# A two-layer hybrid decoder trunk on one core: keys carried in DRAM, a fifth weight-pair tile, and a last output projection that goes block by block

## The chip, the cores and the metric

The kernel runs on one core of a Trainium2 chip. The metric is the device time of one execution in microseconds; the time before is the median of three runs. TensorE is called PE below, VectorE DVE, ScalarE ACT, GpSimd POOL, and SyncE SP. SP issues every DMA of this kernel, in one queue, in order.

## The reference, cut to what matters

Two layers run over 2048 positions of width 1024. In each layer the same input feeds sliding-window attention (16 query heads in 4 key/value groups, window 128) and a Mamba-2 chunked scan (16 heads in 2 groups, 128 states, chunks of 128 positions). Their outputs, each gated with SiLU, are concatenated and go through one output projection; the result is added to the scaled input and layer-normalised.

```python
def hybrid_layer(x, w_in, ..., w_out, ln_g, ln_b):
    proj = jnp.einsum("bld,de->ble", x, w_in)
    q, k, v, z_attn, z_ssm, xbc, dt_raw = jnp.split(proj, IN_SPLITS, axis=-1)
    attn = sliding_window_attention(q, k, v, sinks) * jax.nn.silu(z_attn)
    ...
    y = ssd_chunked(xs, dt, a, bm, cm)
    ...
    ssm = gated_rmsnorm(y, z_ssm, ssm_norm_w)
    out = jnp.einsum("ble,ed->bld", jnp.concatenate([attn, ssm], axis=-1), w_out)
    return layer_norm(DEEPNORM_ALPHA * x + out, ln_g, ln_b)
```

## The kernel before

**Chunks, halves, blocks.** A layer L goes through four chunks c of 512 positions. A chunk has two halves; each half does two of the four key/value groups and one of the two scan groups. Work on tokens goes in four blocks b of 128 positions.

**Parts and pairs.** Every float32 matmul operand is held as a high part and a low part in a 32-bit matmul format, and a product is three matmuls: high by high, high by low, low by high (lines 236 to 238, 244 to 246, 480 to 482). Both parts of a piece of a weight lie side by side in one tile, `wpair`, 4 KB for each partition; four of them rotate. A pair serves twelve matmuls of 512 columns. In layer 0 the parts are made on first use, or ahead of use by `w_ahead` for layer 1 (raw weights come into `wr`, the parts go out to DRAM); later uses load 512 KB of ready parts (`w_split`, line 126). The load can be issued only when the matmuls that read the tile's former content are done.

**Order of a half.** `stage_k` projects two groups of keys; `proj_a` projects queries and gates; the output projection of the half before that was put aside (`late`, `tail`) is flushed; `mix_a` does attention for one group, block by block, twice; `proj_s` projects the scan's inputs; `out_proj` projects the attention output (grp 0 or 1); `mix_s` runs the scan over the four blocks, one after the other because a state is carried; its output projection (grp 2 or 3) is `tail`. After the second half `norm_store` does the layer norm.

**The keys.** A `kt` tile holds the parts of one group's keys: 128 columns of the chunk before, then 512 of this one. There are two such tiles. The last 128 columns are copied by ACT into a tile that stays, `kcar` (line 327, the name `kc` in the trace), and copied back into the next chunk's tile by POOL (line 322).

**The mixer's tiles.** What `mix_a` and `mix_s` hand to the output projection are the parts in `mixt`, four tiles, one for each block. A `mix_s` block's tile is the one that the attention output of the same half had, so its content can be written (line 623) once both column halves dh of `out_proj` have read the block.

**The end.** For the last half of the last chunk of the last layer `tail` runs `out_proj` for the first 512 output columns of all four blocks (line 769, `dhs=1`), and then `last_out`: four pairs of the second column half are loaded, three of them into the query tiles `q`, which are free by then; for each block the twelve matmuls of the second half, the addition into `racc`, and the layer norm, whose statistics need both halves (lines 674 to 702). The factor `rstd` of the gated norm is made for all four blocks at once, after the last block of `mix_s` (lines 624 to 627).

**What sets the order.** The program is written in the order above, and a planner then orders each engine's instructions by a simulated timeline (line 44): of what is ready in its simulation, what stands earlier in the program goes first. On the chip each engine keeps that order, SP's queue of DMAs among them. So an instruction that is late on the chip holds up all that stands behind it on its engine, and a change of the number of tiles moves instructions everywhere.

**On-chip memory.** The four `kcar` tiles take 1 KB of a partition each, as much together as one `wpair` tile.

Of the kernel before, what the change touches and what calls it, by code (L numbers as in the profile page):

```python
# [31 lines left out]
P = 128  # L32
# [3 lines left out]
CH = 512  # L36
# [19 lines left out]
def trunk(ctx, tc, a):  # L56
# [16 lines left out]
    def bank(pool, name):  # L73
        if pool is ps_pj:
            return pool.tile([P, 512], F32, name=name, tag="bank")
        tag = TAG[name]
        return pool.tile([P, 512], F32, name=name, tag=tag, bufs=NS if tag == "s" else 1)
# [10 lines left out]
        nc.sync.dma_start(out=t if len(src.shape) == 2 else t.rearrange("p (k n) -> p k n", k=src.shape[1]), in_=src)  # L88
        return t

    kcar = [const.tile([P, 2, P], F32R, name=f"kc{i}") for i in range(4)]
    state = [const.tile([P, 512], F32, name=f"st{i}") for i in range(2)]
    halo = const.tile([P, 12, 3], F32, name="halo")

# [24 lines left out]
    def w_split(key, c, dsrc, n, scale=None, pool=False, dst=None):  # L119

        if dst is None:
            dst = wp.tile([P, 2, WP], F32R, name="wpair", bufs=4)
        d = dst[:, :, 0:n]
        hs, ls = d[:, 0], d[:, 1]
        if key in w_dram:
            nc.sync.dma_start(out=d.bitcast(F32), in_=w_dram[key])
            cnt["use"] += 1
            if cnt["use"] % 3 == 0 and ahead:
                w_ahead(*ahead.pop(0))
            return hs, ls  # L130
        src = w_load(dsrc, n)
        cnt["w"] += pool
        w_parts(hs, ls, src, scale, nc.gpsimd if pool and cnt["w"] % 2 == 0 else nc.vector)
        if key[1] > 0 or not on_use(key):
            nc.sync.dma_start(out=w_store(key, n), in_=d.bitcast(F32))
        return hs, ls
# [175 lines left out]
    def stage_k(L, c, pr, X):  # L312
        ps = bank(ps_cm, "ps_k")
        proj_cm(X, L, pr, ps, pool=False)
        kts = []
        for i in range(2):
            kv = 2 * pr + i
            kt = ap_.tile([P, 2, P + CH], F32R, name="kt", bufs=2)
            kf = kt.bitcast(F32)
            s, o = (slice(0, 64), slice(64, 128)) if i == 0 else (slice(64, 128), slice(0, 64))  # L320
            if c > 0:
                nc.gpsimd.tensor_copy(out=kt[:, :, 0:P], in_=kcar[kv].bitcast(F32))
            nc.scalar.copy(out=kt[s, 0, P:], in_=ps[s])
            nc.vector.tensor_tensor(out=kt[s, 1, P:], in0=ps[s], in1=kf[s, 0, P:], op=ALU.subtract)
            nc.scalar.copy(out=kt[o, 0, P:], in_=ps[s])
            nc.vector.tensor_copy(out=kt[o, 1, P:], in_=kf[s, 1, P:])
            nc.scalar.copy(out=kcar[kv], in_=kf[:, :, CH:CH + P])
            kts.append(kt)
        return kts

# [136 lines left out]
    def new_mixt():  # L467
        return [xp.tile([P, 2, 4, P], F32R, name="mixt", bufs=4) for _ in range(NB)]

    def out_proj(L, c, grp, mixt, racc, evac, nw=None, pre=None, dhs=2):  # L470
        for dh in range(dhs):
            if pre is not None:
                pre(dh)
            banks = [bank(ps_acc, "ps_out") for _ in range(NB)]
            for e in range(4):
                wh, wl = w_split(("o", L, grp, dh, e), c, a["wo"][L, grp, dh][:, e, :], 512,
                                 None if nw is None else nw[:, e:e + 1])
                for b in range(NB):
                    mh, ml = mixt[b][:, 0, e, :], mixt[b][:, 1, e, :]
                    nc.tensor.matmul(out=banks[b], lhsT=mh, rhs=wh, start=(e == 0), stop=False)  # L480
                    nc.tensor.matmul(out=banks[b], lhsT=mh, rhs=wl, start=False, stop=False)  # L481
                    nc.tensor.matmul(out=banks[b], lhsT=ml, rhs=wh, start=False, stop=(e == 3))  # L482
            for b in range(NB):
                evac(b, racc[b][:, dh * 512:(dh + 1) * 512], banks[b])
# [63 lines left out]
        o["zs"] = [silu2(banks[b], sp.tile([P, 512], F32, name="zss", bufs=4)) for b in range(NB)]  # L548
        return o

    def mix_s(L, lc, c, g, d, o, mixt):
        ssq = sm.tile([P, NB], F32, name="ssq")
        for b in range(NB):
            blk = slice(b * P, (b + 1) * P)
            hs = slice(b * 16 + g * 8, b * 16 + g * 8 + 8)
# [65 lines left out]
            for e in range(4):  # L621
                nc.tensor.transpose(out=pg[:, e * P:(e + 1) * P], in_=y[:, e * P:(e + 1) * P], identity=ident)
            split(mixt[b][:, 0], mixt[b][:, 1], pg.rearrange("p (e t) -> p e t", e=4), "act")
        rstd = sm.tile([P, NB], F32, name="rstd")
        nc.vector.tensor_scalar(out=rstd, in0=ssq, scalar1=1.0 / 2048, scalar2=EPS, op0=ALU.mult, op1=ALU.add)
        nc.gpsimd.tensor_tensor(out=rstd, in0=rstd, in1=mhalf, op=ALU.pow)
        nc.vector.tensor_scalar(out=rstd, in0=rstd, scalar1=0.5, scalar2=None, op0=ALU.mult)
        return rstd

    def norm_store(L, c, racc):  # L630
# [27 lines left out]
    def last_out(L, c, grp, mixt, racc, rstd, nw):  # L658

        gb = []  # L660
        for i in range(2):
            gb.append([])
            for n in ("lng", "lnb"):
                t = sp.tile([P, CH], F32, name="cacc", bufs=4) if i == 0 else wp.tile([P, 512], F32, name=n, tag="wr", bufs=4)
                nc.sync.dma_start(out=t, in_=a[n][L][:, i * 512:(i + 1) * 512])
                gb[i].append(t)
        w = []
        for e in range(4):
            w.append(w_split(("o", L, grp, 1, e), c, a["wo"][L, grp, 1][:, e, :], 512, nw[:, e:e + 1],
                             dst=ap_.tile([P, 2, CH], F32R, name="q", bufs=3) if e < 3 else None))  # L670
        for b in range(NB):
            r = racc[b]
            st = sm.tile([P, 2, 6], F32, name="bst")
            nc.vector.bn_stats(out=st[:, 0, :], in_=r[:, 0:512])
            ps = bank(ps_acc, "ps_out")
            for e, (wh, wl) in enumerate(w):
                mh, ml = mixt[b][:, 0, e, :], mixt[b][:, 1, e, :]
                nc.tensor.matmul(out=ps, lhsT=mh, rhs=wh, start=(e == 0), stop=False)
                nc.tensor.matmul(out=ps, lhsT=mh, rhs=wl, start=False, stop=False)
                nc.tensor.matmul(out=ps, lhsT=ml, rhs=wh, start=False, stop=(e == 3))  # L680
            ev_rstd(rstd)(b, r[:, 512:], ps)
            nc.vector.bn_stats(out=st[:, 1, :], in_=r[:, 512:])
            mv = sm.tile([P, 2], F32, name="bmv")
            nc.vector.bn_aggr(out=mv, in_=st)
            rs = sm.tile([P, 1], F32, name="brs")
            nc.vector.tensor_scalar(out=rs, in0=mv[:, 1:2], scalar1=EPS, scalar2=None, op0=ALU.add)
            nc.gpsimd.tensor_tensor(out=rs, in0=rs, in1=mhalf[:, 0:1], op=ALU.pow)
            nm = sm.tile([P, 1], F32, name="bnm")
            nc.vector.scalar_tensor_tensor(out=nm, in0=mv[:, 0:1], scalar=-1.0, in1=rs, op0=ALU.mult, op1=ALU.mult)
            for i in (1, 0):  # L690
                cs = slice(i * 512, (i + 1) * 512)
                h = r[:, cs]
                if i == 1:
                    nc.scalar.activation(out=h, in_=h, func=AF.Identity, scale=rs, bias=nm)
                    nc.gpsimd.tensor_tensor(out=h, in0=h, in1=gb[i][0], op=ALU.mult)
                    eng = nc.vector if b > 0 else nc.gpsimd
                    eng.tensor_tensor(out=h, in0=h, in1=gb[i][1], op=ALU.add)
                else:
                    nc.vector.scalar_tensor_tensor(out=h, in0=h, scalar=mv[:, 0:1], in1=gb[i][0], op0=ALU.subtract,
                                                   op1=ALU.mult)  # L700
                    nc.vector.scalar_tensor_tensor(out=h, in0=h, scalar=rs, in1=gb[i][1], op0=ALU.mult, op1=ALU.add)
                nc.sync.dma_start(out=a["out"][c * CH + b * P:c * CH + (b + 1) * P, cs], in_=h)
# [32 lines left out]
    for L in range(DEPTH):  # L735
# [3 lines left out]
        for c in range(NCH):  # L739
# [7 lines left out]
            for half in range(2):  # L747
# [12 lines left out]
                    Xn = XLoad(L + (c + 1) // NCH, (c + 1) % NCH)  # L760
                    pre = Xn.half
                out_proj(L, c, half, mixt, racc, ev_alpha if half == 0 else ev_add, pre=pre)
                mixt = new_mixt()
                rstd = mix_s(L, lc, c, half, d, o, mixt)

                def tail(L=L, c=c, half=half, mixt=mixt, racc=racc, rstd=rstd, lc=lc):
                    end = half == 1 and L == DEPTH - 1 and c == NCH - 1
                    nw = lc["nw"][:, half * 4:half * 4 + 4]
                    out_proj(L, c, 2 + half, mixt, racc, ev_rstd(rstd), nw, dhs=1 if end else 2)
                    if end:  # L770
                        last_out(L, c, 2 + half, mixt, racc, rstd, nw)
                    elif half == 1:
                        norm_store(L, c, racc)

                late.append(tail)
# [60 lines left out]
```

## Time and profile before

| what | us |
|---|---|
| median of 3 runs | 3191.21 |
| lowest and highest run | 3185.13, 3192.55 |
| the profiled execution, its own time | 3184.89 |
| its span, first to last instruction | 3182.9 |
| PE busy | 3079.0 (97%) |
| DVE, ACT, POOL busy | 2153.3, 1612.5, 1365.2 |
| granted TensorE clock, mean | 0.991 of full |

The profile is of one execution. Times in the trace count from its first instruction. PE's busy time is made of modelled ends, so that of matmuls that follow each other the steps from start to start count, and not the length of one. "Released by" stands for the instruction or DMA that ended a wait.

### The profile page before, as it was taken

What the parts mean: (1) busy time and instruction counts of PE and PEld (TensorE: products, weight loads), DVE (VectorE), ACT (ScalarE), POOL (GpSimd) and SP (SyncE); (2) the same over time, 40 slices, a digit from 0 to 9 for tenths busy, and PEclk for the clock granted to TensorE, in tenths of its full rate; (3) what the DMA queues carried; (4) which work ended last, traced back from release to release, by engine and by line L of the source; (5) the groups of instructions that cost most, each with busy time, mean ns of one, the idle gap of its engine ahead of it and who ended that gap; (6) DMA issues with size and microseconds to landing.
All of it is one profiled execution on the core that took longest, in us unless ns stands there. A gap on an engine that the chain in (4) does not pass through costs nothing.

```text
span 3182.9 us, 48382 instructions
## 1 busy us (share of the span) xinstructions
PE 3079.0 (97%) x15704; PEld 2577.9 (81%) x15704; DVE 2153.3 (68%) x4686; ACT 1612.5 (51%) x4599; POOL 1365.2 (43%) x1967
## 2 busy tenths in 40 slices
PE   8999999999998999999999999999999999999996
PEld 7878787878877788877888888888888888888885
DVE  5877768676686676866757676675766747666475
ACT  5746537455373553645536464372643636335362
POOL 2554534425354253542535434444344433455234
PEclk9999999999999999999999999999999999999998
DMA  8657759496594864957556556765556545575452
GB/s 312 233 189 247 248 172 318 150 316 211 170 322 145 289 228 155 326 188 268 189 159 226 176 193 190 229 201 166 180 173 235 183 159 185 168 229 181 152 196 79
DMA packets 254461, 663.58 MB, mean 208 GB/s; under 512 B 28288, under 2 KB 49408, under 8 KB 254208
## 3 DMA queue, kind: packets, MB, share of 16 engines
q1 hardware_dynamic: 254208, 660.49, 62.4%
q8 instruction: 124, 2.03, 0.3%
q14 instruction: 129, 1.06, 0.1%
HBM read 534.02 MB, written 126.35 MB: 207 GB/s over the span
## 4 chain that ended last, share of the span: by engine, by line
PE 71%; DMA 15%; DVE 5%; POOL 3%; ACT 3%; issue 2%; SPq 1%; DVEq 0%; ACTq 0%; POOLq 0%
PE ps_out L480 6%; PE ps_out L482 6%; PE ps_out L481 6%; PE ps_xbc L238 3%; PE ps_xbc L236 3%; PE ps_xbc L237 3%; PE ps_q L236 3%; PE ps_q L238 3%; PE ps_q L237 3%; PE ps_yd L581 3%; PE ps_z L238 3%; PE ps_z L236 3%; PE ps_z L237 3%; DMA wr<-wcm 3%; PE ps_zs L244 3%; PE ps_zs L245 2%
## 5 line engine op out<-in xcount | busy, mean ns | idle before, releaser
L480 PE MATMUL ps_out<-wpair,mixt 128*128 128x512 f32 x1008 | 395.4, 401 | 26.3 <-DMA wpair<-wd_o 13.3
L482 PE MATMUL ps_out<-wpair,mixt 128*128 128x512 f32 x1008 | 397.1, 396 | 7.2 <-DVE mixt L105 4.0
L481 PE MATMUL ps_out<-wpair,mixt 128*128 128x512 f32 x1008 | 396.8, 394 | 0.4 <-DVE wpair L105 0.4
L414 ACT ACTIVATE e<-e,nm 128x129 f32<-128x129 f32 x512 | 202.7, 397 | 219.5 <-DVE nm L410 218.9
L236 PE MATMUL ps_xbc<-xh,wpair 128*128 128x512 f32 x768 | 305.2, 397 | 0.6 <-DMA wpair<-wd_cm 0.5
L238 PE MATMUL ps_xbc<-xh,wpair 128*128 128x512 f32 x768 | 303.6, 395 | 0.0
L237 PE MATMUL ps_xbc<-xl,wpair 128*128 128x512 f32 x768 | 302.3, 394 | 0.0
L435 POOL TENSOR_SCALAR_AFFINE_SELECT gh<-fh 64x256 fp32r<-64x256 f32 x256 | 110.3, 431 | 333.4 <-ACT fh L100 325.0
L480 PEld LDWEIGHTS ps_out<-wpair,mixt 128*128 128x128 f32 x1008 | 191.0, 191 | 72.6 <-DMA wpair<-wd_o 17.2
L574 ACT ACTIVATE e<-e,nacs 128x128 f32<-128x128 f32 x512 | 163.7, 392 | 161.3 <-DVE e L572 155.0
L482 PEld LDWEIGHTS ps_out<-wpair,mixt 128*128 128x128 f32 x1008 | 191.3, 190 | 50.7 <-DVE mixt L105 6.3
L526 DVE SCALAR_TENSOR_TENSOR cacc<-ps_xbc,conv,cacc 128x511 f32<-128x511 f32 (+2 forms) x288 | 213.1, 740 | 23.5 <-ACT cacc L523 22.0
L481 PEld LDWEIGHTS ps_out<-wpair,mixt 128*128 128x128 f32 x1008 | 191.8, 190 | 38.7 <-DVE wpair L105 0.8
L244 PE MATMUL ps_zs<-wpair,xh 128*128 128x512 f32 x512 | 205.0, 403 | 8.5 <-DMA wpair<-wd_z 7.9
L236 PE MATMUL ps_q<-xh,wpair 128*128 128x512 f32 x512 | 201.4, 393 | 2.8 <-DMA wpair<-wd_cm 1.5
L246 PE MATMUL ps_zs<-wpair,xl 128*128 128x512 f32 x512 | 202.7, 397 | 0.0
L245 PE MATMUL ps_zs<-wpair,xh 128*128 128x512 f32 x512 | 202.6, 396 | 0.0
L236 PE MATMUL ps_z<-xh,wpair 128*128 128x512 f32 x512 | 201.8, 394 | 0.0
L238 PE MATMUL ps_z<-xh,wpair 128*128 128x512 f32 x512 | 201.7, 394 | 0.0
L238 PE MATMUL ps_q<-xh,wpair 128*128 128x512 f32 x512 | 200.5, 392 | 0.8 <-DVE wpair L105 0.8
L237 PE MATMUL ps_z<-xl,wpair 128*128 128x512 f32 x512 | 200.8, 392 | 0.0
L237 PE MATMUL ps_q<-xl,wpair 128*128 128x512 f32 x512 | 200.8, 392 | 0.0
(219 smaller groups left out, 8287.6 us busy)
## 6 DMA issues: line engine op xcount, KB each, us to landing
wpair<-wd_cm SPq DMA_DIRECT2D x420, 512.0 KB, 4.0
wpair<-wd_o SPq DMA_DIRECT2D x157, 512.0 KB, 3.9
wpair<-wd_z SPq DMA_DIRECT2D x112, 512.0 KB, 4.2
e<-a SPq DMA_DIRECT2D x128, 256.0 KB, 3.9
wr<-wcm SPq DMA_DIRECT2D x120, 256.0 KB, 4.5
wd_cm<-wpair SPq DMA_DIRECT2D x60, 512.0 KB, 3.5
wr<-wo SPq DMA_DIRECT2D x112, 256.0 KB, 4.7
wd_o<-wpair SPq DMA_DIRECT2D x32, 512.0 KB, 3.8
```

The source lines that it names most:

```text
L236: nc.tensor.matmul(out=ps, lhsT=wh[:, s], rhs=xh, start=(k == 0), stop=False)
L237: nc.tensor.matmul(out=ps, lhsT=wh[:, s], rhs=xl, start=False, stop=False)
L238: nc.tensor.matmul(out=ps, lhsT=wl[:, s], rhs=xh, start=False, stop=(k == KT - 1))
L244: nc.tensor.matmul(out=banks[b], lhsT=xh[:, s], rhs=wh, start=(k == 0), stop=False)
L245: nc.tensor.matmul(out=banks[b], lhsT=xh[:, s], rhs=wl, start=False, stop=False)
L246: nc.tensor.matmul(out=banks[b], lhsT=xl[:, s], rhs=wh, start=False, stop=(k == KT - 1))
L414: nc.scalar.activation(out=s5[:, h, :], in_=s5[:, h, :], func=AF.Exp, scale=-1.0, bias=nm[:, h:h + 1], accum_out=den[:, h:h + 1])
L480: nc.tensor.matmul(out=banks[b], lhsT=mh, rhs=wh, start=(e == 0), stop=False)
L481: nc.tensor.matmul(out=banks[b], lhsT=mh, rhs=wl, start=False, stop=False)
L482: nc.tensor.matmul(out=banks[b], lhsT=ml, rhs=wh, start=False, stop=(e == 3))
L526: nc.vector.scalar_tensor_tensor(out=acc[:, m:], in0=ps[:, 0:CH - m], scalar=cw[:, j:j + 1], in1=acc[:, m:], op0=ALU.mult, op1=ALU.add)
L574: nc.scalar.activation(out=e4[:, h, :], in_=e4[:, h, :], func=AF.Exp, scale=-1.0, bias=nacs[:, h:h + 1])
```

## The change

Four edits. The keys' last 128 columns go to a DRAM tile by DMA and come back by DMA, one of two tiles for each group by turns, instead of the copies by ACT and POOL. `wpair` has five tiles. For the last half alone the mixer's `mixt` tiles are cut out of two tiles of the name `xh`, which held the high parts of the layer's input, and `rstd` is made for each block when the block is done. The last output projection does not begin with the first column half of all blocks; `last_out` loads all eight pairs (five of them in `wpair`, three in `q`) and does for each block both column halves, and then its layer norm.

```diff
-    kcar = [const.tile([P, 2, P], F32R, name=f"kc{i}") for i in range(4)]
+    k_dram = [[dram.tile([P, 2, P], F32, name=f"k{kv}_{i}") for i in range(2)] for kv in range(4)]
...
-            dst = wp.tile([P, 2, WP], F32R, name="wpair", bufs=4)
+            dst = wp.tile([P, 2, WP], F32R, name="wpair", bufs=5)
...
             if c > 0:
-                nc.gpsimd.tensor_copy(out=kt[:, :, 0:P], in_=kcar[kv].bitcast(F32))
+                nc.sync.dma_start(out=kf[:, :, 0:P], in_=k_dram[kv][(c + 1) % 2])
...
-            nc.scalar.copy(out=kcar[kv], in_=kf[:, :, CH:CH + P])
+            if c < NCH - 1:
+                nc.sync.dma_start(out=k_dram[kv][c % 2], in_=kf[:, :, CH:CH + P])
...
+    def last_mixt():
+        t = [xp.tile([P, 4, CH], F32R, name=f"xh{i}").rearrange("p (b e) t -> p b (e t)", b=2) for i in range(2)]
+        return [t[b // 2][:, b % 2].rearrange("p (s e t) -> p s e t", s=2, e=4) for b in range(NB)]
...
-    def mix_s(L, lc, c, g, d, o, mixt):
+    def mix_s(L, lc, c, g, d, o, mixt, end=False):
         ssq = sm.tile([P, NB], F32, name="ssq")
+        rstd = sm.tile([P, NB], F32, name="rstd")
+        def scale(s):
+            nc.vector.tensor_scalar(out=rstd[:, s], in0=ssq[:, s], scalar1=1.0 / 2048, scalar2=EPS, op0=ALU.mult,
+                                    op1=ALU.add)
+            nc.gpsimd.tensor_tensor(out=rstd[:, s], in0=rstd[:, s], in1=mhalf[:, s], op=ALU.pow)
+            nc.vector.tensor_scalar(out=rstd[:, s], in0=rstd[:, s], scalar1=0.5, scalar2=None, op0=ALU.mult)
...
+            if end:
+                scale(slice(b, b + 1))
+        if not end:
+            scale(slice(0, NB))
         return rstd
...
-        for e in range(4):
-            w.append(w_split(("o", L, grp, 1, e), c, a["wo"][L, grp, 1][:, e, :], 512, nw[:, e:e + 1],
-                             dst=ap_.tile([P, 2, CH], F32R, name="q", bufs=3) if e < 3 else None))
+        for dh in range(2):
+            for e in range(4):
+                t = ap_.tile([P, 2, CH], F32R, name="q", bufs=3) if dh and e < 3 else None
+                w.append(w_split(("o", L, grp, dh, e), c, a["wo"][L, grp, dh][:, e, :], 512, nw[:, e:e + 1], dst=t))
         for b in range(NB):
...
-            nc.vector.bn_stats(out=st[:, 0, :], in_=r[:, 0:512])
-            ps = bank(ps_acc, "ps_out")
-            for e, (wh, wl) in enumerate(w):
...
+            for dh in range(2):
+                ps = bank(ps_acc, "ps_out")
+                for e, (wh, wl) in enumerate(w[4 * dh:4 * dh + 4]):
...
+                h = r[:, dh * 512:dh * 512 + 512]
+                ev_rstd(rstd)(b, h, ps)
+                nc.vector.bn_stats(out=st[:, dh, :], in_=h)
...
+                end = half == 1 and L == DEPTH - 1 and c == NCH - 1
+                mixt = last_mixt() if end else new_mixt()
+                rstd = mix_s(L, lc, c, half, d, o, mixt, end)
...
-                    out_proj(L, c, 2 + half, mixt, racc, ev_rstd(rstd), nw, dhs=1 if end else 2)
                     if end:
                         last_out(L, c, 2 + half, mixt, racc, rstd, nw)
-                    elif half == 1:
+                        return
+                    out_proj(L, c, 2 + half, mixt, racc, ev_rstd(rstd), nw)
+                    if half == 1:
                         norm_store(L, c, racc)
```

## Rows read from the trace of the kernel before

**Rows 1.** The page: its first line, and PE's busy time, share, instructions.

```profile
span 3182.9 us, 48382 instructions
PE 3079.0 (97%) x15704; PEld 2577.9 (81%) x15704; DVE 2153.3 (68%) x4686; ACT 1612.5 (51%) x4599; POOL 1365.2 (43%) x1967
```

**Rows 2.** Windows: stretch, length, busy of PE, PEld, DVE, ACT, POOL; clock, DMA share, GB/s.

```profile
818.50:1225.50 407.00, 387.93 (x1951) 320.46 (x1950) 283.14 (x613) 210.13 (x594) 173.09 (x246) 0.99 0.69 230
2004.60:2390.40 385.80, 382.12 (x1984) 322.96 (x1983) 255.05 (x571) 188.13 (x552) 166.86 (x246) 1.00 0.59 192
3087.20:3163.80 76.60, 67.56 (x304) 54.77 (x302) 39.34 (x60) 18.96 (x46) 34.40 (x33) 0.91 0.26 90
```

**Rows 3.** PE's waits, whole span: for whom, us in total, times, longest.

```profile
PE ps_out L480 <- DMA wpair<-wd_o: 13.3, 12, 2.4
PE ps_zs L244 <- DMA wpair<-wd_z: 7.9, 3, 3.5
```

**Rows 4.** Windows of the clock's falls: three in layer 0, one near the end.

```profile
534.70:538.10 3.40, 3.40 (x11) 2.84 (x12) 1.06 (x4) 2.07 (x7) 1.80 (x5) 0.50 1.03 404
729.20:736.10 6.90, 6.24 (x17) 5.17 (x18) 2.86 (x9) 2.43 (x7) 1.28 (x1) 0.51 0.83 302
1370.90:1374.40 3.50, 3.50 (x10) 2.72 (x11) 0.40 (x1) 1.85 (x7) 2.84 (x4) 0.51 1.04 397
...
3125.40:3132.20 6.80, 6.56 (x24) 5.92 (x25) 2.17 (x4) 1.56 (x3) 3.38 (x4) 0.50 0.00 0
```

**Rows 5.** Timeline of SP, then of PE, at the longest of these waits.

```profile
717.75 5.75 SPq L88 DMA_DIRECT2D wr<-wo  x4
723.60 0.85 SPq L126 DMA_DIRECT2D wpair<-wd_z  x2
...
729.86 0.80 PE L244 MATMUL ps_zs<-wpair,xh 128*128 128x512 f32 x1 [3.48 <-DMA wpair<-wd_z]
```

**Rows 6.** The page's DMA issues: count, KB each, us from issue to landing.

```profile
wpair<-wd_o SPq DMA_DIRECT2D x157, 512.0 KB, 3.9
```

**Rows 7.** Timeline of PE: two starts, ten matmuls of 512 columns apart.

```profile
3084.72 0.39 PE L245 MATMUL ps_zs<-wpair,xh 128*128 128x512 f32 x1
...
3086.99 0.39 PE L246 MATMUL ps_zs<-wpair,xl 128*128 128x512 f32 x1
```

**Rows 8.** Lines: the keys' two copies; busy, mean ns, idle before.

```profile
L327 ACT CAST kc<-kt 128x256 fp32r<-128x256 f32 x32 | 12.9, 404 | 5.2 <-DVE kt L326 4.8
L322 POOL CAST kt<-kc 128x256 fp32r<-128x256 f32 x24 | 11.6, 482 | 7.0 <-PE ps_s L397 5.9
```

**Rows 9.** Waits of SP's own queue: the bias load and a pair's store.

```profile
SPq L135 <- DVE wpair L105: 76.1, 39, 8.4
SPq L378 <- DVE nm L410: 66.5, 27, 7.2
```

**Rows 10.** Timeline of the end: last mixer block, last matmul, last block's norm.

```profile
3149.81 0.69 DVE L105 TENSOR_TENSOR mixt<-ps_g,mixt 128x512 fp32r<-128x512 f32 x1 [0.41 <-ACT mixt L100]
...
3163.34 0.39 PE L680 MATMUL ps_out<-wpair,mixt 128*128 128x512 f32 x1
...
3171.54 0.14 DVE L686 TENSOR_SCALAR brs<-bmv 128x1 f32<-128x1 f32 x1
...
3174.97 0.54 POOL L687 TENSOR_TENSOR brs<-brs,mhalf 128x1 f32<-128x1 f32 x1
```

**Rows 11.** Lines of the window from 3160 to 3183: the layer norm's parts.

```profile
L695 POOL TENSOR_TENSOR racc<-racc,lng 128x512 f32<-128x512 f32 x4 | 6.1, 1538 | 2.2 <-ACT racc L694 2.2
...
L687 POOL TENSOR_TENSOR brs<-brs,mhalf 128x1 f32<-128x1 f32 x4 | 3.5, 874 | 15.2 <-DVE brs L686 15.2
...
L712 DVE SCALAR_TENSOR_TENSOR racc<-ps_out,rstd,racc 128x512 f32<-128x512 f32 x4 | 2.9, 732 | 4.9 <-PE ps_out L680 4.9
L682 DVE BATCH_NORM_STATS2 bst<-racc 128x6 f32<-128x512 f32 x4 | 2.7, 678 | 0.0
```

**Rows 12.** One line's instructions, whole span: ns least, median, most.

```profile
L617 POOL TENSOR_TENSOR yy<-yy,zss x64: 1264/1619/1739, 176.7 to 3147.2; 128x512 f32<-128x512 f32 x64
```

More of the change, by code (lines that the diff above doesn't have):

```diff
@@ L468, in new_mixt, with out_proj @@
         return [xp.tile([P, 2, 4, P], F32R, name="mixt", bufs=4) for _ in range(NB)]
-    def out_proj(L, c, grp, mixt, racc, evac, nw=None, pre=None, dhs=2):
-        for dh in range(dhs):
+    def last_mixt():
+        t = [xp.tile([P, 4, CH], F32R, name=f"xh{i}").rearrange("p (b e) t -> p b (e t)", b=2) for i in range(2)]
+        return [t[b // 2][:, b % 2].rearrange("p (s e t) -> p s e t", s=2, e=4) for b in range(NB)]
+    def out_proj(L, c, grp, mixt, racc, evac, nw=None, pre=None):
+        for dh in range(2):
             if pre is not None:
@@ L623, in mix_s @@
             split(mixt[b][:, 0], mixt[b][:, 1], pg.rearrange("p (e t) -> p e t", e=4), "act")
[L624 to L627, printed above, removed]
+            if end:
+                scale(slice(b, b + 1))
+        if not end:
+            scale(slice(0, NB))
         return rstd
@@ L673, in last_out @@
             st = sm.tile([P, 2, 6], F32, name="bst")
-            nc.vector.bn_stats(out=st[:, 0, :], in_=r[:, 0:512])
-            ps = bank(ps_acc, "ps_out")
-            for e, (wh, wl) in enumerate(w):
[L677 to L682, printed above, removed]
+            for dh in range(2):
+                ps = bank(ps_acc, "ps_out")
+                for e, (wh, wl) in enumerate(w[4 * dh:4 * dh + 4]):
+                    mh, ml = mixt[b][:, 0, e, :], mixt[b][:, 1, e, :]
+                    nc.tensor.matmul(out=ps, lhsT=mh, rhs=wh, start=(e == 0), stop=False)
+                    nc.tensor.matmul(out=ps, lhsT=mh, rhs=wl, start=False, stop=False)
+                    nc.tensor.matmul(out=ps, lhsT=ml, rhs=wh, start=False, stop=(e == 3))
+                h = r[:, dh * 512:dh * 512 + 512]
+                ev_rstd(rstd)(b, h, ps)
+                nc.vector.bn_stats(out=st[:, dh, :], in_=h)
             mv = sm.tile([P, 2], F32, name="bmv")
@@ L762, in trunk, with tail @@
                 out_proj(L, c, half, mixt, racc, ev_alpha if half == 0 else ev_add, pre=pre)
[L763 to L767, printed above, removed]
+                end = half == 1 and L == DEPTH - 1 and c == NCH - 1
+                mixt = last_mixt() if end else new_mixt()
+                rstd = mix_s(L, lc, c, half, d, o, mixt, end)
+                def tail(end=end, L=L, c=c, half=half, mixt=mixt, racc=racc, rstd=rstd, lc=lc):
                     nw = lc["nw"][:, half * 4:half * 4 + 4]
-                    out_proj(L, c, 2 + half, mixt, racc, ev_rstd(rstd), nw, dhs=1 if end else 2)
                     if end:
                         last_out(L, c, 2 + half, mixt, racc, rstd, nw)
-                    elif half == 1:
+                        return
+                    out_proj(L, c, 2 + half, mixt, racc, ev_rstd(rstd), nw)
+                    if half == 1:
                         norm_store(L, c, racc)
```

## The prediction

> **What bounds the kernel now.** I read the page first. PE is busy for 3079.0 of 3182.9 us [rows 1], so only the rest can go: the waits of PE, and what runs after its last matmul. No edit takes a matmul away. The windows say where the rest lies. A chunk of layer 0 takes 407.0 us with PE busy for 387.9, a chunk of layer 1 385.8 with 382.1 [rows 2]: layer 1 has under 4 us a chunk to give, layer 0 about 19. The end is worst. From 3087.2, where the last output projections begin, to the last matmul's end at 3163.8, PE works 67.6 of 76.6 us at a mean clock of 0.91 [rows 2], and after that 19.1 us pass without a matmul (3182.9 − 3163.8). PE's waits by releaser then tell which of them the change can reach: weight pairs that landed late made up 13.3 us in the output projections and 7.9 in the scan's gate, 21.2 together; the loads of other pairs are under 2 us a line [rows 3]. Last I read SP's queue before such a wait, the two copies of the keys, and the end's timeline.
>
> **The fifth pair tile.** A pair serves twelve matmuls. Ten starts stand 2.27 us apart, so a pair lasts 12 × 0.227 = 2.72 us [rows 7]. With four tiles, a tile that comes free must be filled within the 3 × 2.72 = 8.2 us of the other three, with five within 10.9. A load takes 3.9 us from issue to landing [rows 6], so the tiles suffice, if SP issues at once. In layer 0 it does not: ahead of the longest wait four loads of raw weights held the queue for 5.75 us, and the pair's load behind them went out at 723.60 [rows 5]; PE, which had waited for 3.48 us, began with it at 729.86 [rows 5]. With a fifth tile the planner can place the same load one pair earlier, ahead of such entries, and the slack grows by 2.72 us. No wait for the output projection's pairs is above 2.4 us and the longest for the gate's is 3.5 [rows 3], so all but a fraction could go. Three of the waits are followed by a stretch at half clock (1.2 instead of 2.4 GHz) of 3.4, 6.9 and 3.5 us [rows 4], in which half the time is lost: 6.9 us. The most that the tile can give is thus 21.2 + 6.9 = 28 us, the least is nothing, because the queue is newly ordered and other entries may come to stand ahead of the loads. I take half, 14 us: the row that is nearest, the wait before 729.86 [rows 5], would be shortened by 2.72 of 3.5 us, but not every load will stand earlier.
>
> **The keys.** Removed: 32 copies on ACT, 12.9 us, and 24 on POOL, 11.6 us [rows 8]. ACT is busy for 51% and POOL for 43% of the span [rows 1], PE is not seen waiting for either copy; I count nothing, at most 3 us (a fraction of the 5.9 us that POOL stood waiting to copy). Added: 24 loads and 24 stores of 128 KB on SP, each in the same queue as the pairs. A load waits until the last score matmul has read the old tile; queued behind it on SP are the pairs that PE needs next. The trace has no such DMA. Its nearest row is the bias load, whose tile is freed by the instruction that reads those same scores: 27 waits, 66.5 us, 2.5 each, the longest 7.2 [rows 9]. The new wait ends just before one that SP makes anyway. A store waits for the last copy of the keys; nearest is a pair's store, 76.1 us over 39, 2.0 each [rows 9]. With five tiles SP may stand still for 10.9 − 3.9 = 7.0 us before PE notices, nearly the longest bias wait. So the cost is from nothing to, at the worst, 24 × 2.5 = 60 us if no wait were covered; I take 2 us, near the lower end because of that cover. The keys themselves come tens of microseconds before their first use, as the tile is free that early.
>
> **The end, up to PE's last matmul.** Before, the high part of the last mixer block is ready at 3149.8 [rows 10], and 14.0 us of matmuls still follow until 3163.8, because one column half of the other blocks was left for then. Now only the 24 matmuls of the last block follow: 24 × 0.227 = 5.4 us, so 8.6 us less, if the mixer blocks come as now. The bounds: if the last matmuls fall into a stretch at half clock, as there is one at 3125.4 [rows 4], they take 10.9 us and 3.1 is left. Upwards, PE's idle time of 9.0 us and the clock's loss, (1 − 0.91) × 76.6 = 6.9 us [rows 2], could all go, 16 us. Downwards, POOL now does the norms of blocks 0 to 2 beside the mixer: two powers of 0.87 us and one product of 1.54 a block [rows 11], 3.3 × 3 = 10 us, and if all of that delayed the mixer the last matmul would come 1 us later than before. What hides it is that POOL is busy for only 34.4 of 76.6 us there [rows 2]. The extra three sets of `rstd` are in this sum.
>
> **The end, after the last matmul.** The 19.1 us are four norms that reached DVE together. Now one is left. Its chain: addition 0.73 and statistics 0.68 [rows 11], two small operations and a hand-over to POOL, 0.5, and from the power at 3174.97 to the end 7.9 [rows 10], which has the power, the ACT step, product, addition and store; 9.8 us, say 10. The other bound is the last block as it ran among the others: 3182.9 − 3171.5 = 11.4 from its line 686, with 1.6 ahead of it 13. So 9 us less (6 to 9). Together with the 8.6 us the end gives 17.6; I take 16, since the norms of earlier blocks will not be entirely hidden.
>
> **A rule against it.** The same product on POOL takes 1.26 us at the least and 1.62 as a median over the span [rows 12], so POOL's work is stretched by what runs beside it, and the new norms run beside the mixer. The Trainium skill, "SBUF — State Buffer", section "Who interferes with whom", says that a DVE instruction with two SBUF inputs and a GpSimd instruction that reads SBUF share a read interface, and one of them waits for the whole of the other. By this rule three DVE steps of each of three norms, 0.73 us each as on line 712 [rows 11], would stand in POOL's way, 6.6 us, and the sum below would be 21 instead of 28. I stay with the row: a stretch of 0.36 us an instruction on an engine that is idle for half the window.
>
> **The sum.** 14 − 2 + 16 = 28 us. The profiled execution took 3184.9 us (its span 3182.9 and 2.0 around it) and would take 3157. The median of the runs shown is 6.3 us above it, so the forecast for the median is 3191.2 − 28 = 3163 us. The planner's new order moves small waits (PE's idle time but for the pairs and the end: 3182.9 − 3079.0 − 21.2 − 19.1 = 64 us [rows 1, 3]) up and down; I give that 8 us to both sides.
>
> **The rivals.**
> The fifth tile gives nothing. For it: the loads stand behind entries that wait for other things [rows 5], and the planner, which thinks its queue is on time, may put them there again. Against it: in layer 1 the same wait comes without such entries, when the four tiles come free together. Then −16 + 2 = −14, 3177 us. Chance 0.20.
> The mixer is slowed by the norms. For it: rows 12 and the order of work on POOL and DVE, which is fixed and not chosen on the chip. Then the end gives 16 − 9 = 7, and the sum is −19, 3172 us. Chance 0.13.
> The new mixer tiles don't do what they should: two blocks share one `xh` tile, and if the framework takes a block's write to touch the other's reads, a block's parts wait for the former block's 24 matmuls, 3 × 5.4 = 16 us. The end then gives nothing, −12, 3179 us. Against it: slices of `racc` and `kt` are used side by side now. Chance 0.06.
> Slower: the keys' loads stop SP's queue. Place: layer 0's and layer 1's attention, at the change of a `kt` tile. It decides from the point where SP stands for more than 7.0 us with the entries behind it, which the bias waits reach only at their longest [rows 9]; in layer 0 the queue is also slow by itself. Price: the 12 loads there each stop PE for 2.5 us and bring a half-clock stretch of 3.4 [rows 4], so 12 × (2.5 + 1.7) = 50, with no gain from the tile: +50 − 16 = +34, 3225 us. Chance 0.09.
> All of it: end 22, tile 28: −50, 3141 us. Chance 0.07.
>
> **How the numbers follow.** The forecast, 3163 us, has 0.45; its own range, with the planner's 8 us and the bounds of tile and end, is 3150 to 3178. The range for 8 in 10 runs from 3142 to 3190: it takes in the other faster cases and leaves out the slower one and part of the best. About 0.3%, 9.6 us, is what a measurement of this kernel can tell from no change, so faster begins below 3181.6. The forecast and the best case are faster; of the 0.20 for the tile half is; of the 0.13 for the mixer 0.11; of the 0.06 half: 0.76, of which I keep 0.75. The same: 0.08 + 0.02 + 0.03, 0.14 with what I kept. Slower: 0.09 and 0.02 of the tile's rival, 0.11.
>
> **What would show it.** In PE's waits the rows for `wd_o` and `wd_z` fall from 21.2 us to about 10, and the half-clock stretches of layer 0 go from three to one or two. In SP's waits the new rows of the keys are near 2.5 us each. At the end the four blocks' last matmuls lie some 10 us apart instead of together, and from the last matmul to the end of the span there are about 10 us instead of 19.1. The prediction is wrong if PE waits for pairs as long as now, if it waits behind the keys, or if the last mixer block is ready more than 8 us later, counted from the first output projection, than the 62.6 us of before (3149.8 − 3087.2).

## The result, and the profile after

The changed kernel took 3155.3 us (median of four runs) against 3191.9 us for the kernel before on the same chip: ratio 0.9884, 95% interval 0.9868 to 0.9900, 37 us less. Beside the experiments it was timed again: 3151.1 against 3189.1 us, ratio 0.9874 (0.9861 to 0.9887), 38 us less by the medians and 40 by the ratio. The forecast was 3163 us, 28 less. Direction and range held; the gain was larger than forecast.

Single executions of one kernel differ here by 10 to 17 us, and the two profiles are an unequal pair: the one of before was among the fastest of its kernel (3184.9 us), the first one of after the slowest of its four (3162.3 us). A second profile of the changed kernel has 3152.1 us. Where time went is therefore read from several profiles, and how much from the timed ratios.

The page of the changed kernel begins so; PE's work is what it was [rows 1].

```profile
span 3160.5 us, 48519 instructions
...
PE 3081.4 (97%) x15704; PEld 2580.8 (82%) x15704; DVE 2150.5 (68%) x4692; ACT 1600.3 (51%) x4567; POOL 1368.5 (43%) x1946
```

PE's waits in the changed kernel (for whom, us in total, times, longest). The second line and the third, of the keys' projection, are all that is left of the waits for weight pairs: the output projections' and the gate's were 13.3 and 7.9 us before [rows 3], and are 3.3 and nothing now. The first line has grown: PE waited 5.6 us for the same POOL masking before, and 15.1 now.

```profile
PE ps_o L451 <- POOL fl L436: 15.1, 23, 1.5
...
PE ps_out L486 <- DMA wpair<-wd_o: 3.3, 3, 1.4
...
PE ps_k L236 <- DMA wpair<-wd_cm: 1.1, 1, 1.1
```

SP's own waits: the bias load, then the keys' store, then the three kinds of wait before the keys' load. The loads waited for 17.4 us in these three kinds and for 19.2 in all, 0.8 a load over 24; the stores' row is 1.8 us a wait over 19. The bias load's wait fell [rows 9].

```profile
SPq L379 <- DVE nm L411: 40.8, 24, 3.1
...
SPq L328 <- DVE kt L326: 34.8, 19, 4.6
...
SPq L322 <- PE ps_xt L503: 5.9, 3, 2.7
SPq L322 <- PE ps_s L398: 5.8, 5, 1.5
SPq L322 <- PE ps_xbc L238: 5.7, 2, 2.8
```

The end as a window, from the last gate matmul to the last matmul (length, busy PE, PEld, DVE, ACT, POOL, clock, DMA share, GB/s), and as a timeline. The window has 72.7 us for 76.6 [rows 2], with DVE at 48.8 for 39.3: the norms of the first blocks are now inside it. In the timeline the powers of the four norms (line 703) lie 14, 12 and 7 us apart. The last block's high part is begun at 3144.51, the last matmul ends at 3151.5, and 9.0 us later the span is over, instead of 19.1 [rows 10]. In the second profile the window has 69.2 us.

```profile
3078.80:3151.50 72.70, 65.90 (x303) 52.90 (x302) 48.75 (x85) 21.43 (x49) 42.38 (x43) 0.93 0.30 104
```

```profile
3120.41 1.00 POOL L703 TENSOR_TENSOR brs<-brs,mhalf 128x1 f32<-128x1 f32 x1
...
3134.32 0.99 POOL L703 TENSOR_TENSOR brs<-brs,mhalf 128x1 f32<-128x1 f32 x1 [0.56 <-DVE brs L702]
...
3144.51 0.59 ACT L100 CAST xh<-ps_g 128x512 fp32r<-128x512 f32 x1 [0.77 <-PE ps_g L636]
...
3146.21 0.55 POOL L703 TENSOR_TENSOR brs<-brs,mhalf 128x1 f32<-128x1 f32 x1
...
3151.10 0.39 PE L695 MATMUL ps_out<-wpair,xh 128*128 128x512 f32 x1
...
3153.52 0.99 POOL L703 TENSOR_TENSOR brs<-brs,mhalf 128x1 f32<-128x1 f32 x1 [3.92 <-DVE brs L702]
```

### The profile page after: what moved, and what is told of

Same layout as the page of the kernel before. It is cut to its first block, busy times and chain, and to the rows that moved or that the text cites. A ratio compares the mean times of both kernels' runs of the same rounds, so it can differ in the third digit from the quotient of the medians.

```text
span 3160.5 us, 48519 instructions
## 1 busy us (share of the span) xinstructions
PE 3081.4 (97%) x15704; PEld 2580.8 (82%) x15704; DVE 2150.5 (68%) x4692; ACT 1600.3 (51%) x4567; POOL 1368.5 (43%) x1946
## 4 chain that ended last, share of the span: by engine, by line
PE 71%; DMA 12%; DVE 6%; ACT 5%; POOL 4%; issue 2%; SPq 0%; POOLq 0%; DVEq 0%; ACTq 0%
PE ps_out L486 6%; PE ps_out L487 6%; PE ps_out L488 6%; PE ps_xbc L236 3%; PE ps_xbc L237 3%; PE ps_xbc L238 3%; DMA wr<-wcm 3%; DMA e<-a 3%; PE ps_z L238 3%; PE ps_z L237 3%; PE ps_z L236 3%; PE ps_q L236 3%; PE ps_q L238 3%; PE ps_q L237 3%; PE ps_yd L595 3%; DMA wd_cm<-whi 3%
## 5 line engine op out<-in xcount | busy, mean ns | idle before, releaser
L486 PE MATMUL ps_out<-wpair,mixt 128*128 128x512 f32 x992 | 390.8, 401 | 9.5 <-DMA wpair<-wd_o 3.3
L487 PE MATMUL ps_out<-wpair,mixt 128*128 128x512 f32 x992 | 390.1, 394 | 0.7 <-DVE wpair L105 0.7
L488 PE MATMUL ps_out<-wpair,mixt 128*128 128x512 f32 x992 | 387.7, 394 | 0.0
L486 PEld LDWEIGHTS ps_out<-wpair,mixt 128*128 128x128 f32 x992 | 188.8, 191 | 51.3 <-DMA wpair<-wd_o 4.5
L488 PEld LDWEIGHTS ps_out<-wpair,mixt 128*128 128x128 f32 x992 | 188.0, 190 | 39.3
L487 PEld LDWEIGHTS ps_out<-wpair,mixt 128*128 128x128 f32 x992 | 188.6, 190 | 38.5 <-DVE wpair L105 1.6
```

## The experiments

In each group the kernels shared the runs of the kernel before; ratios are against it, 0.001 of a ratio is 3.2 us, and a gain given in us is worked out from the ratio.

### One edit, or two, at a time

**The end alone.** Keys and tiles as before; the eighth pair goes to a key tile, which is free by then.

```diff
 (changed kernel, keys and wpair as before)
-                t = ap_.tile([P, 2, CH], F32R, name="q", bufs=3) if dh and e < 3 else None
+                t = None
+                if dh:
+                    t = ap_.tile([P, 2, CH], F32R, name="q", bufs=3) if e < 3 else ap_.tile([P, 2, P + CH], F32R, name="kt", bufs=2)[:, :, 0:CH]
```

> The end alone: keys stay in SBUF (copies by ACT and POOL), four pair tiles as before; the last mixer's tiles in xh and the block-by-block end are as in the changed kernel, with the eighth pair of weights in a free kt tile. My theory (the three edits add up; the end gives some 17 us): 17 us faster than before, between 12 and 20, ratio 0.995; from the last matmul to the end of the span about 9 to 10 us instead of 19.1; PE's waits for weight pairs stay near 20 us. Rival (the end needs the fifth tile, because eight pairs are wanted at once and four tiles let them land too late): less than 6 us faster, with PE waiting for pairs inside the last output projection.

Measured: 3175.3 us, ratio 0.9952 (0.9938 to 0.9965), 15 us faster. From the last matmul (its end at 3168.8) to the end of the span 9.0 us. PE waits for pairs as before:

```profile
PE ps_out L485 <- DMA wpair<-wd_o: 11.4, 10, 2.4
PE ps_zs L244 <- DMA wpair<-wd_z: 7.4, 4, 2.5
```

The end does not need the fifth tile.

**Keys and fifth tile, the end as before.**

```diff
 (kernel before)
-            dst = wp.tile([P, 2, WP], F32R, name="wpair", bufs=4)
+            dst = wp.tile([P, 2, WP], F32R, name="wpair", bufs=5)
 (and the keys in DRAM as in the change)
```

> Keys in DRAM and five pair tiles, the end as before. My theory: 18 us faster, between 12 and 25, because PE's waits for weight pairs fall from 21 us to under 6; from the last matmul to the end 19 us as before. Rival (the gain of the changed kernel is all in the end, and a new order of the body only trades one wait for another): within 5 us of before, with other waits of PE up by what the pairs' waits went down.

Measured: 3162.1 us, ratio 0.9909 (0.9896 to 0.9923), 29 us faster. PE's waits for pairs are nearly gone; the wait for POOL's masking has grown here too:

```profile
PE ps_o L451 <- POOL fl L436: 15.4, 22, 1.5
...
PE ps_out L481 <- DMA wpair<-wd_o: 4.4, 2, 2.5
```

One expectation failed: from the last matmul to the end it took 12.1 us, not 19, though nothing was changed there.

**Keys alone, four tiles.**

```diff
 (kernel before; wpair keeps bufs=4)
-                nc.gpsimd.tensor_copy(out=kt[:, :, 0:P], in_=kcar[kv].bitcast(F32))
+                nc.sync.dma_start(out=kf[:, :, 0:P], in_=k_dram[kv][(c + 1) % 2])
 (and the store, as in the change)
```

> Keys in DRAM, four pair tiles, the end as before. My theory: no gain, 0 to 5 us slower, PE's waits for pairs as before or a few us longer, since the keys' DMAs stand in SP's queue without a larger cover. Rival one (it is the copies taken off ACT and POOL that help): 5 us or more faster with the pairs' waits unchanged. Rival two (the keys' loads stop SP's queue and the fifth tile only hides it): 15 us or more slower, PE's waits for pairs above 30 us.

Measured: 3192.6 us, ratio 1.0005 (0.9996 to 1.0014): no change that can be told, 1.3 us faster to 4.5 slower. Both rivals fall as they were stated, 5 us faster and 15 slower. A small gain from the copies and a small cost of the DMAs could still cancel in this time.

```profile
PE ps_out L481 <- DMA wpair<-wd_o: 13.5, 10, 2.6
PE ps_o L451 <- POOL fl L436: 9.2, 22, 1.2
...
PE ps_zs L244 <- DMA wpair<-wd_z: 6.3, 4, 3.3
```

So nearly all that keys and tile gain together is the tile's: with the keys in DRAM in both, five tiles for four give 31 us (29.0 and 1.6). The memory is the point of moving the keys; a fifth tile with the keys on the chip was not tried.

**The changed kernel again.**

> The changed kernel once more, beside the others on one chip, for an interval and a second profile. All theories: ratio 0.986 to 0.991. If the three edits add up, its gain is that of the end alone plus that of keys and pair together, within 5 us; if they overlap, it is less.

Measured: 0.9874 (0.9861 to 0.9887). The parts sum to 15.3 + 29.0 = 44 us, the whole is 37 and 40. Each of these figures has 4 to 5 us to either side, so by the times alone they may overlap by 4 to 7 us or not at all. The traces say that they do: keys and tile alone had already shortened the tail, from 19 to 12 us.

### What in the end counts

**The last mixer's tiles put back.**

```diff
 (changed kernel)
-                mixt = last_mixt() if end else new_mixt()
+                mixt = new_mixt()
```

> The changed kernel, but the last mixer's tiles are the ones that the attention output had, as before; block by block, keys and fifth pair stay. My theory (the gain of the end comes from the block order, and the mixer's blocks are paced by their own chain of states): as the changed kernel within 4 us, some 36 us faster than before. Rival (the mixer has to wait for the attention output's projection to free its tiles, and that is what the end was short of): 6 us or more slower than the changed kernel, with the first block's transposes (line 636) 5 us or more later after the mixer product than in the changed kernel.

Measured: 3149.3 us, ratio 0.9879 (0.9865 to 0.9892), the same as the changed kernel. The tiles are not waited for. The timeline shows the first block's gated product, its transposes directly behind it, and directly behind those the first write into the tile:

```profile
3092.23 1.62 POOL L631 TENSOR_TENSOR yy<-yy,zss 128x512 f32<-128x512 f32 x1
...
3093.91 0.66 PE L636 MATMUL ps_g<-ident,yy 128*128 128x128 f32 x4 [0.42 <-POOL yy L631]
...
3094.60 0.59 ACT L100 CAST mixt<-ps_g 128x512 fp32r<-128x512 f32 x1
```

**The tiles moved, the old end.**

```diff
 (keys and fifth tile, the end as before)
-                mixt = new_mixt()
+                mixt = last_mixt() if half == 1 and L == DEPTH - 1 and c == NCH - 1 else new_mixt()
```

> Keys in DRAM, five pair tiles, the last mixer's tiles in xh, but the last output projection as before (first column half of all blocks, then block by block). My theory: as with keys and pair alone, 29 us faster than before, within 4. Rival (the tiles are what counts): as the changed kernel, 36 to 40 us faster.

Measured: 3159.6 us, ratio 0.9907 (0.9893 to 0.9920), as without the tiles. What counts at the end is the block order.

**One line: the eighth pair in a key tile, all else as before.** With four tiles the eighth pair, the fifth to go into `wpair`, had to wait until one of the four was free: its load was issued at 3152.87. In the timeline of the kernel before, its matmuls are the last of every block:

```profile
3152.87 0.32 SPq L126 DMA_DIRECT2D wpair<-wd_o  x1
...
3159.71 0.39 PE L678 MATMUL ps_out<-wpair,mixt 128*128 128x512 f32 x1
...
3160.39 0.39 PE L678 MATMUL ps_out<-wpair,mixt 128*128 128x512 f32 x1
...
3161.07 0.39 PE L678 MATMUL ps_out<-wpair,mixt 128*128 128x512 f32 x1
...
3162.88 0.39 PE L678 MATMUL ps_out<-wpair,mixt 128*128 128x512 f32 x1
```

So all four blocks end within 4 us, and their norms queue on DVE; three of the four powers there (the last is in [rows 10]):

```profile
3164.81 0.98 POOL L687 TENSOR_TENSOR brs<-brs,mhalf 128x1 f32<-128x1 f32 x1 [14.31 <-DVE brs L686]
3166.71 0.99 POOL L687 TENSOR_TENSOR brs<-brs,mhalf 128x1 f32<-128x1 f32 x1 [0.92 <-DVE brs L686]
...
3172.70 0.98 POOL L687 TENSOR_TENSOR brs<-brs,mhalf 128x1 f32<-128x1 f32 x1
```

```diff
 (kernel before)
-                             dst=ap_.tile([P, 2, CH], F32R, name="q", bufs=3) if e < 3 else None))
+                             dst=ap_.tile([P, 2, CH], F32R, name="q", bufs=3) if e < 3 else
+                             ap_.tile([P, 2, P + CH], F32R, name="kt", bufs=2)[:, :, 0:CH]))
```

> The kernel before with one line changed: the last of the eight pairs of weights goes to a free kt tile instead of a fifth use of wpair. My new theory (the one pair that had to wait for a tile until the first column half was nearly done kept the last three matmuls of all four blocks together at the end, and the fifth tile undid this): 7 us faster than before, between 4 and 10, and 12 to 14 us from the last matmul to the end of the span instead of 19.1. Rival (the end got shorter with keys and pair because the whole order changed): within 3 us of before and 18 to 20 us after the last matmul.

Measured: the norms come apart (timeline below), and 12.8 us are left after the last matmul, as expected. But the time is 3186.0 us, ratio 0.9995 (0.9984 to 1.0006): at most 5 us faster, perhaps nothing, which is what the rival had for the time. In its one profile the end is 5.6 us shorter and the way to it 5.5 us longer, though PE's order there is that of before. The mechanism at the end is shown by the trace; its worth in time is not.

```profile
3163.03 0.99 POOL L688 TENSOR_TENSOR brs<-brs,mhalf 128x1 f32<-128x1 f32 x1 [6.24 <-DVE brs L687]
...
3167.82 1.00 POOL L688 TENSOR_TENSOR brs<-brs,mhalf 128x1 f32<-128x1 f32 x1
...
3172.50 0.98 POOL L688 TENSOR_TENSOR brs<-brs,mhalf 128x1 f32<-128x1 f32 x1 [0.59 <-DVE brs L687]
3174.70 0.92 POOL L688 TENSOR_TENSOR brs<-brs,mhalf 128x1 f32<-128x1 f32 x1 [1.22 <-DVE brs L687]
```

### What the keys cost, and what a tile is worth

**Every DMA of the keys twice.**

```diff
 (changed kernel)
                 nc.sync.dma_start(out=kf[:, :, 0:P], in_=k_dram[kv][(c + 1) % 2])
+                nc.sync.dma_start(out=kf[:, :, 0:P], in_=k_dram[kv][(c + 1) % 2])
...
                 nc.sync.dma_start(out=k_dram[kv][c % 2], in_=kf[:, :, CH:CH + P])
+                nc.sync.dma_start(out=k2_dram[kv][c % 2], in_=kf[:, :, CH:CH + P])
```

> The changed kernel with every DMA of the keys issued twice: the load twice into the same place, the store also to a second DRAM tile that nobody reads. My theory (the keys' DMAs wait beside waits that SP makes anyway, under the cover of five tiles): 0 to 4 us slower than the changed kernel. Rival (each entry in SP's queue costs PE something, and the gain of the changed kernel is net of it): 48 more entries cost 8 us or more.

Measured: 3155.9 us, ratio 0.9899 (0.9886 to 0.9912). Against the kernel with the old mixer tiles of the same group, which is as fast as the changed one, it is 6.5 us slower, between what the two theories said; the intervals overlap. PE's waits for pairs went up to 9.7 us:

```profile
PE ps_out L489 <- DMA wpair<-wd_o: 9.7, 7, 2.1
```

So 48 more entries probably cost a few microseconds; this is not settled to better than that.

**Three tiles.**

```diff
 (keys alone)
-            dst = wp.tile([P, 2, WP], F32R, name="wpair", bufs=4)
+            dst = wp.tile([P, 2, WP], F32R, name="wpair", bufs=3)
```

> Keys in DRAM, three pair tiles, the end as before. My theory (what the tile gives is the time for which SP's queue may stand still: 7.0 us with five tiles, 4.2 with four, 1.5 with three): PE's waits for pairs rise from 23 us with four tiles to 80 us or more, and the kernel is 60 us or more slower than before. Rival (the fifth tile helped by a luckier order, not by its cover): within 25 us of before.

Measured: 3214.8 us, ratio 1.0073 (1.0055 to 1.0091), 23 us slower, not 60. The waits for pairs are 37 us in all (three largest below), not 80.

```profile
PE ps_xbc L236 <- DMA wpair<-wd_cm: 10.6, 15, 2.6
PE ps_out L481 <- DMA wpair<-wd_o: 10.5, 10, 1.9
PE ps_zs L244 <- DMA wpair<-wd_z: 10.2, 11, 4.2
```

The time lies where the rival had it, within 25 us of before. The order of three, four and five tiles (37, 23 and 5 us of waits, 23 us and 2 us slower and 29 us faster, all with the keys in DRAM) is that of the cover, the time for which SP's queue may stand still. The cover's arithmetic made too much of it, so a part of the fifth tile's gain may be a better order. The planner knows the number of tiles and may put other work where a pair would be late; that is a guess.

**Six tiles, and the control.** The place comes from one raw-weight tile and one `e4` tile; the control gives these up too and keeps five.

```diff
 (changed kernel; the control has the first two of these changes and keeps bufs=5)
-            t = wp.tile([P, WP], F32, name="wr", bufs=4)        (and its other uses)
+            t = wp.tile([P, WP], F32, name="wr", bufs=3)
-E4 = 4
+E4 = 3
-            dst = wp.tile([P, 2, WP], F32R, name="wpair", bufs=5)
+            dst = wp.tile([P, 2, WP], F32R, name="wpair", bufs=6)
```

> The changed kernel with six pair tiles; the place for the sixth is taken from the raw weights (three tiles instead of four) and from the decay and score tiles e4 (three instead of four). To be read against the same trimming with five tiles. My theory (five tiles have left 4 us of waits for pairs, so the cover is used up): 0 to 5 us faster than the trimmed kernel with five. Rival (a tile is worth its whole 22 us again, since the tile gave more than the waits it removed): 10 us or more faster than that.

> The changed kernel with three raw-weight tiles and three e4 tiles, five pair tiles: the control for the kernel with six. All theories: 0 to 20 us slower than the changed kernel, mostly in layer 0 where raw weights are loaded, and no faster.

Measured: six tiles 3232.5 us, ratio 1.0131 (1.0112 to 1.0150); the control 3228.3 us, 1.0115 (1.0095 to 1.0135). The sixth tile gives nothing that can be told. In the one profile of each, PE waits 4.1 us for pairs with six tiles and 10.6 in the control, so a few microseconds of waits went and no time with them. The trimming costs 75 us against the changed kernel, far more than the 20 that I allowed: the two tiles given up are worth more together than the fifth pair tile. Which of the two it is was not tried, nor a sixth tile without the trimming.

**Two more steps at the end.**

```diff
 (changed kernel; the eighth pair in a kt tile as above, and)
-                if i == 1:
+                if i == 1 and b < NB - 1:
```

> The changed kernel with two more steps of the same kind at the end: the eighth pair of weights lies in a free kt tile, so that wpair has one to spare, and the last block's norm does both halves on DVE instead of one by ACT, POOL and DVE. My theory: 1 to 5 us faster than the changed kernel, with 7.5 to 8.5 us after the last matmul instead of 9.0. Rival (the end is paced by the mixer's chain of states, and nothing is left to win behind it): within 1 us.

Measured: 7.6 us after the last matmul instead of 9.0, as meant, and 3151.2 us, ratio 0.9881 (0.9862 to 0.9899): no different from the changed kernel. 1.4 us cannot be told in this measurement, and no version here is faster than the changed kernel by more than the noise.

## Why the prediction was right, and where it was short

The profiles put side by side, in us. The first column of times is from the first instruction to the last gate matmul (`ps_zs`) of the last half, the next from there to the end of the span, the last all of PE's waits for pairs. Behind the last gate matmul PE has the same 303 matmuls in all of them.

| kernel | pair tiles | to the last gate matmul | from there | after the last matmul | waits for pairs |
|---|---|---|---|---|---|
| before | 4 | 3087.4 | 95.5 | 19.1 | 25 |
| keys alone | 4 | 3093.3 | 98.3 | 19.2 | 23 |
| end alone | 4 | 3096.8 | 81.0 | 9.0 | 23 |
| eighth pair in a key tile | 4 | 3092.9 | 89.9 | 12.8 | 25 |
| keys and fifth tile | 5 | 3068.3 | 90.3 | 12.1 | 5 |
| tiles moved, old end | 5 | 3062.4 | 90.4 | 12.1 | 4 |
| changed | 5 | 3078.8 | 81.7 | 9.0 | 4 |
| changed, second profile | 5 | 3072.2 | 78.2 | 9.0 | 4 |
| changed, old mixer tiles | 5 | 3067.2 | 79.0 | 9.0 | 4 |
| keys twice | 5 | 3070.4 | 83.4 | 9.0 | 10 |
| two more steps | 5 | 3086.5 | 77.6 | 7.6 | 4 |

**The fifth tile: the step that was too small.** "I take half, 14 us … not every load will stand earlier". Nearly every wait went. The waits for pairs fell by some 20 us in the profiles with five tiles (13 to 15 with the keys' DMAs doubled), and the way to the last gate matmul is on average 20 us shorter (3092.6 in the four profiles with four tiles, 3072.3 in the seven with five; single ones scatter by 10 us and more, and the last line reaches the others). Much of that scatter is the clock: the stretches at half clock up to this matmul add up to 14 to 44 us in these profiles, and with half of their time taken off, an estimate, the four lie at 3074 to 3081 and the seven at 3054 to 3064. By time, keys and tile together gave 29 us (25 to 33), and keys alone nothing. So my upper bound of 28 was about the value, by chance, for it was made of the wrong things: I counted 6.9 us of half clock as recoverable, but half-clock stretches are as frequent after as before (to the last gate matmul 27 us before, 37 and 27 us in the two profiles of the changed kernel; in layer 0 there were seven before, of which I named the three behind waits for pairs, and there are eight and five now); and I left out what the tile does at the end, where the eighth pair no longer comes late and 5 to 8 us went (90.3 against 95.5 and 98.3).

**The keys.** Two microseconds were taken, with a worst case of 60; measured −1.3 to 4.5, with the copies' gain in it. The loads waited 0.8 us each instead of the 2.5 of the nearest row: there are 14 waits for 24 loads, and the view of their line shows no instruction that waits for one to land. The store's row was well chosen: 1.8 us for 2.0. What I did not see: PE's wait for the masking grew from 5.6 to 9.2 us with keys alone and to 15 with five tiles. It is 7.9 us with only the eighth pair moved and 10.7 with the keys' DMAs doubled, so its cause is not shown; a new order by the planner is likely.

**The end.** Sixteen taken; 15.3 by itself (11 to 20), and 11 on top of keys and tile, which had taken a part of the tail already. The tail went to 9.0 us, forecast 10. From the last block's high part (ready at 3145.1) to the end of the last matmul it took 6.4 us, and 5.8 in the second profile, against 13.9 before [rows 10]; 5.4 was the bare sum of matmuls. That part is ready 66.3 and 63.4 us after the last gate matmul, 3.7 and 0.8 later than the 62.6 of before, where 8 would have spoken against the prediction. The 11 us show in the traces too, against keys and fifth tile with the old end. There the last block's high part comes 62.2 us after the last gate matmul, and 16.0 us of matmuls follow:

```profile
3129.89 0.58 ACT L100 CAST mixt<-ps_g 128x512 fp32r<-128x512 f32 x1 [0.45 <-PE ps_g L623]
...
3146.10 0.39 PE L681 MATMUL ps_out<-wpair,mixt 128*128 128x512 f32 x1
```

So the new end saves 10 us up to the last matmul and 3 us behind it, and loses 1 to 4 because the mixer is later.

**The rule against it.** The mixer's gated products of the four blocks end 37.9 us apart, first to last, in the kernel before, and 37.6 us in the changed one (35.5 in its second profile), with three norms beside them. But these kernels differ in their tiles too. With five tiles and the old end the products end 33.8 us apart in both kernels, with five tiles and the new end 35.5 to 37.6 in four profiles (39.0 with the keys' DMAs doubled); with four tiles it is 37.9 to 39.3 with the old end and 40.1 with the new. So at five tiles the mixer is 2 to 4 us slower beside the new end, where the sum allowed 1.6. One product takes what it took [rows 12]:

```profile
L631 POOL TENSOR_TENSOR yy<-yy,zss x64: 1264/1622/1842, 185.0 to 3141.7; 128x512 f32<-128x512 f32 x64
```

The 6.6 us that would follow from the rule of the Trainium skill, "SBUF — State Buffer", section "Who interferes with whom", are thus not reached in those four profiles. Whether an instruction was ever held is not told by these rows, and the output matmuls that now stand between the mixer's on PE could slow it as well; what did is open.

**The rivals.** The fifth tile gives nothing: excluded by 29 us. The mixer is slowed by the norms: not by the 9 us of the rival; it is 2 to 4 us slower, from a cause that is open. The moved tiles serialise the blocks: no, and they don't help either. The keys stop SP's queue: no.

## What to carry to other kernels

When a queue that issues loads in order makes the main engine wait, first ask how long the queue may stand still before it is noticed (tiles ahead times the time of one, less the landing): one more tile took away 20 of 25 us of waits here, and a sixth gave no time. That sum tells the direction and not the price: for three tiles it said 60 us or more, and 23 came. Memory for it is best taken from what is used rarely and early known, as the keys were; taking it from tiles in constant use cost 75 us, where the fifth tile had given some 30. And where several blocks share a last resource, look which operand comes last for all of them: work that ends together queues on the next engine, and finishing block by block hides all of that but the last block's share behind the next block's matmuls.

## What the runs showed that was not expected

SP needs 0.56 us to issue a keys' DMA (median of the 24 stores, which have two runs of 512 bytes a partition) and 0.32 us for most loads of pairs. Pairs took 4.0 to 4.4 us to land with the keys' DMAs in the queue, 3.9 to 4.2 before.
